# Last expert's PSUM sums moved into its first matrix, and four banks cleared earlier at the start

## The chip, the cores and the metric

One core of a Trainium2 chip runs the whole program. The metric is device time in microseconds (us) of one execution. TensorE's clock has two levels, 1.2 and 2.4 GHz; the profile gives the granted clock as a share of the upper one (0.50 or 1.00).

## The reference

One decoder layer over 256 tokens of width 1024, in float32. Two head groups share one input projection (4 heads of differential attention, 8 heads of RWKV-7 time mixing); then comes a mixture of 32 experts, 4 per token. Norms are modulated by six vectors made from a conditioning vector.

```python
mod = silu(c) @ ada_w + ada_b
sh1, sc1, gt1, sh2, sc2, gt2 = split(mod, 6)
h = rms_norm(x, pre_mix_norm) * (1 + sc1) + sh1
proj = h @ w_in
da_part, rw_part = proj[..., :DA_COLS], token_shift(proj[..., DA_COLS:], rw_mu)
lam = exp(sum(lam_q1 * lam_k1)) - exp(sum(lam_q2 * lam_k2)) + lambda_init
# attention: (softmax(q1 k1) - lam * softmax(q2 k2)) v, for each head
y = concat([diff_attention(da_part), rwkv7_time_mix(rw_part)]) @ w_out
x = x + gt1 * rms_norm(y, post_mix_norm)
h = rms_norm(x, pre_ffn_norm) * (1 + sc2) + sh2
gates = top-4 softmax of (h @ router_w + router_b)
acc = sum over e of gates[e] * (clamped_swiglu(h @ w1[e] + b1[e]) @ w2[e] + b2[e])
return x + gt2 * rms_norm(acc, post_ffn_norm)
```

## The kernel before

Weights stream from HBM through a ring of 18 slots of 1 MB in SBUF. SyncE's queue issues nearly all loads in program order; a load is issued when the slot it writes has been released by the instructions that read it. Tokens are gathered per expert into 32, 64 or 96 columns (`kind`), multiplied with the first matrix (`gemm1`, eight row blocks k of w1, which come as four loads of 2 MB, so k = 0 and 1 arrive together), put through the activation (`act_of`), transposed (`act_tr`), multiplied with the second matrix (`gemm2`, four loads of 1 MB in the order 0, 2, 1, 3), scaled by the gates into `ys`, and put back to their tokens by a matmul with `back` (`scatter`). For most experts VectorE adds the scattered rows to `acc` in SBUF. Both GEMMs take a table `between`: after row block k they call `between[k]`, which is how other work is put into TensorE's queue at a chosen place. TensorE, VectorE and ScalarE take their instructions in exactly this written order in this part of the program.

PSUM has eight banks: four named `bank`, three `bankb` and one `bankc`. For the last expert, the result is summed in PSUM: `sum_so_far(i)` (L1764) takes two banks for token tile i, and puts into each, by a matmul with the identity, what `acc` holds so far, and then by a matmul of `pgT` with `b2t` the gated biases of all second matrices. `b2t` is loaded by GpSimd (L1860) in `late_rows`, when the last expert begins. When a tile has its `ends`, `scatter` adds into these banks and VectorE has nothing to add. `last_norm` then reads them. In the kernel before, the last expert issues `warm(24)` (matmuls of ones, whose result nobody reads) behind its first matrix, and the scatter of the last expert but one and both `sum_so_far` are woven into its second matrix.

At the start, the modulation vectors are computed four times 256 columns at a time: `mod_rows` (products with `cs`, one row in each of four partition groups), `mod_copy` (VectorE copies them to SBUF), `mod_cols_first` (matmuls with `q32` that turn rows into columns, then VectorE makes scale `g1` and shift `sh1`), `mod_x` (ScalarE and VectorE apply them and split the result into a high and a low part). `col_tr(0)` transposes the small parameter vectors `prow` into columns `pc`. `split_first` splits weights in high and low parts. `proj_first` is the projection, accumulated over eight row blocks in seven banks, which are cleared beforehand by a matmul with zeros (`rwb`, L427 to L431).

Lambda of the attention is computed by five VectorE operations and an exponential on ScalarE (L729 to L736) in a part of the program that a scheduler orders; there `tc.issue_after` holds an operation back until a named one was placed.

Of the kernel before, what the change touches and what calls it, by code (L numbers as in the profile page):

```python
# [15 lines left out]
AF = mybir.ActivationFunctionType  # L16
OP = mybir.AluOpType
# [5 lines left out]
NT = 2  # L23
# [8 lines left out]
SINGLE = 4  # L32
# [14 lines left out]
MIX = "hh" "mh" "mh" "hw" + ("mm" "hm" "hw") * 2 + "mm" "mm" "hm" "mm" "hh"  # L47
MAX_OVER = 16
OVER_AT = 8
WARM = (34, 4, 0, 6, 8)  # L50
LEAD = 5
WORK = ("* * * d1 * * d2 * * * d2 * * d2 * d1 * d1 * d3 * T1 d2 T3 * T0 K0.0 d4 U0 d1 * d5 * K0.4 r0 * * T2 d2 m * * "
        "L0.0 d3 U2 K1.0 m * d4 m * q0.0 * L1.0 d4 K1.4 L0.4 d1 m m m r1 d5 d1 m q1.0 d2 q0.1 q1.1 d2 * s0.0 * "
# [22 lines left out]
def hybrid_layer_kernel(ctx, tc, x, c, positions, ada_w, ada_b, pre_mix_norm, post_mix_norm,  # L76
# [335 lines left out]
    xj = pair((1024,), (1024,))  # L412
    norm_x(xj)
    x_tr(0, xj[0])
    mod_rows(0, 0, ada)
    x_tr(1, xj[1])
    mod_rows(0, 1, ada)
    col_tr(0)
    V.tensor_scalar(pc[:, cols["sc1"][0]:cols["sc1"][0] + 8], pc[:, cols["sc1"][0]:cols["sc1"][0] + 8], 1.0, None,
                    op0=OP.add)  # L420
    mod_copy(0)
# [2 lines left out]
    for _ in range(2):  # L424
        next(sf)
    mod_cols_first(0)
    rwb = {}  # L427
    ORDER = (0, 2, 4, 6, 8, 10, 12)
    for f in ORDER:
        rwb[f] = (bankb if f in (12, 8, 10) else bank)()  # L430
        mm(rwb[f], zero, zero[:, 0:1].to_broadcast([128, 512]), True, False)  # L431
    warm(WARM[1], bankc)
    next(sf)
    mod_x(0)
    for _ in sf:
# [6 lines left out]

    mu1 = pro.tile([128, 14], F32)

    def shift(dst, p, f):
        S.activation(dst, p, AF.Copy, scale=mu1[:, f:f + 1])  # L446
        V.scalar_tensor_tensor(dst[:, 1:], p[:, 0:T - 1], col("mu", f), dst[:, 1:], op0=OP.mult, op1=OP.add)  # L447

    def proj_first(k, fs):
# [276 lines left out]
        S.activation(dst[:, :, i * 128:(i + 1) * 128], b.rearrange("p (a b) -> p a b", a=4), AF.Copy)  # L726

    lam2 = pro.tile([128, 2], F32)
    V.tensor_tensor(lamt[:, 0], lamt[:, 0], lamt[:, 1], op=OP.mult)  # L729
    V.tensor_tensor(lamt[:, 2], lamt[:, 2], lamt[:, 3], op=OP.mult)  # L730
    V.tensor_reduce(lam2, lamt[:, 0:4:2], axis=AX.X, op=OP.add)
    with tc.issue_after(first_act.ins):
        S.activation(lam2, lam2, AF.Exp)
    nlam = pro.tile([128, 1], F32)
    V.tensor_tensor(nlam, lam2[:, 1:2], lam2[:, 0:1], op=OP.subtract)
    V.tensor_scalar(nlam, nlam, LAMBDA_INIT, None, op0=OP.subtract)  # L736
    sub_c = pro.tile([128, 1], F32)
    V.tensor_scalar(sub_c, col("subln", 0), 1.0 - LAMBDA_INIT, None, op0=OP.mult)
    scs, ats = {}, {}
# [411 lines left out]
        S.activation(gT[:, f:f + 2], b.rearrange("p (a b) -> p a b", a=2), AF.Copy)  # L1151
    finish(8, 10)
    rkr, gB = rT, gT
    fill()


# [417 lines left out]
        return view(ring[n // 2][:, n % 2], shape)  # L1574


    def load_expert(e, s1_, s2_, single=False):


        w1 = moe_w1[0][e] if isinstance(e, int) else moe_w1[0][bass.ds(e, 1)].rearrange("o k n -> (o k) n")  # L1580
        w2 = moe_w2[0][e] if isinstance(e, int) else moe_w2[0][bass.ds(e, 1)].rearrange("o k n -> (o k) n")
        at = taken[0]
        taken[0] += KC + 4
        for j in range(4):

            d = ring[(at + 2 * j) % N_SLOTS // 2]
            s = w1[j * 256:(j + 1) * 256, :].rearrange("(p k) n -> p k n", k=2)
            s1_ += [d[:, 0], d[:, 1]]
            if j == 3:
                yield  # L1590
            if single:
                nc.sync.dma_start(d[:, 0], s[:, 0])
            if j == 3:
                yield
            if single:
                nc.sync.dma_start(d[:, 1], s[:, 1])
            else:
                nc.sync.dma_start(d.rearrange("p k n -> p (k n)"), s.rearrange("p k n -> p (k n)"))
        for n, k in enumerate(W2_ORDER):
            yield  # L1600
            s = s2_[k] = slot((at + KC + n) % N_SLOTS, (2, D))
            nc.sync.dma_start(s, w2[k * 256:(k + 1) * 256, :].rearrange("(p k) n -> p k n", k=2))

    def load_all(e):
        w = [], {}
# [167 lines left out]

    summed = set()

    def scatter(ys, back, which=range(NT)):
        for i in which:
            for n in range(2):
                h = slice(64 * n, 64 * n + 64)
                if i in ends:  # L1780
                    for m, (j, y) in enumerate(ys):
                        mm(ends[i][n], back[h, j, i], y[h], False, m == len(ys) - 1)
                    continue
                b = bankb()
                for m, (j, y) in enumerate(ys):
                    mm(b, back[h, j, i], y[h], m == 0, m == len(ys) - 1)
                a = acc[:, i, n * 512:(n + 1) * 512]
                if (i, n) in summed:
                    V.tensor_tensor(a, a, b, op=OP.add)  # L1789
                else:  # L1790
                    V.tensor_copy(a, b)
                    summed.add((i, n))
# [130 lines left out]
    for p in range(EXPERTS):  # L1923
        kind = kind_at(p)
        w1s, w2s = weights
        if p + 1 < EXPERTS:
            weights = [], {}
            rest_of_load = load_expert(expert_of(p + 1), *weights, p + 1 < SINGLE)
            next(rest_of_load)
        else:  # L1930
            late_rows()
        between = {}
        if p == 0:
            between = {2: order_a, 4: order_b, 5: order_c, 7: order_d}
        gemm1(bs, xs, w1s, kind, between, rest_of_load)
        act = act_of(bs, kind)
        early = p == 0 or done[2] == 96
# [28 lines left out]

            between[3], between[5] = between[5], rest_of_first
        elif not nxt:
            warm(24)
            between = {0: lambda: scatter(*done[:2], which=(0,)), 1: lambda: scatter(*done[:2], which=(1,)),  # L1970
                       5: lambda: sum_so_far(0), 3: lambda: sum_so_far(1)}
        elif not early:
            scatter(*done[:2], which=(0,))
            if p % 2:
# [10 lines left out]
            over_plan()  # L1985
        if p == OVER_AT:
            last = nc.values_load(n_ov, min_val=0, max_val=MAX_OVER)
    scatter(*done[:2])
    pe_order.close()
    last_norm(ends)  # L1990
    for i in range(NT):
# [64 lines left out]
```

## Time and profile before

| | us |
|---|---|
| median of 3 runs | 1189.94 |
| lowest and highest | 1188.75, 1190.77 |
| the profiled execution | 1190.35 |
| its span, first to last instruction | 1188.5 |
| TensorE busy in the span | 1078.3 |

An interval in the timeline is given as start and length, both in us from the span's start. Busy time of TensorE counts matmuls, also those that run at the lower clock. A time in brackets at a row's end is how long the engine was idle before it and what it waited for.

### The profile page before, as it was taken

To read this page: it belongs to the slowest core of one execution; us is meant where nothing else is said; L and a number is where in the kernel's file an instruction comes from. 1 tells how busy PE (TensorE), PEld (TensorE's weight loads), DVE (VectorE), ACT (ScalarE), POOL (GpSimd) and SP (SyncE) were. 2 spreads that over 40 slices of the span, in tenths; PEclk is the share of its full clock that TensorE was granted. 3 is DMA by queue.
4 is the path that set the end of the run, shared out by engine and by line. 5 is a ranking of instruction groups with operands and counts; after the bars stand their busy time and mean duration, and the time that the engine had idled before them with its cause. 6 is when DMAs were issued, how large, how long until landed. Compare 5 with 4: busy or idle time off the path is not lost.

```text
span 1188.5 us, 17092 instructions
## 1 busy us (share of the span) xinstructions
PE 1078.3 (91%) x6717; PEld 507.3 (43%) x6717; DVE 412.1 (35%) x1114; ACT 227.6 (19%) x529; POOL 53.7 (5%) x100
## 2 busy tenths in 40 slices
PE   8999999999997877999988999988999999798765
PEld 6976667654343232233443233433333434333211
DVE  5688469852331212122323112312212223121203
ACT  4374353312011001010111010111010101101001
POOL 1331020000000000000000000000000000000000
PEclk8999999999999988999999999999999999999978
DMA  9862778899999999999999999999999999999991
GB/s 336 317 235 71 280 270 330 326 371 383 423 424 426 426 425 426 425 426 424 425 425 426 424 426 427 422 426 426 423 426 426 425 426 425 425 426 425 423 382 48
DMA packets 60101, 453.15 MB, mean 381 GB/s; under 512 B 7850, under 2 KB 16105, under 8 KB 23154
## 3 DMA queue, kind: packets, MB, share of 16 engines
q1 hardware_dynamic: 57970, 449.88, 91.9%
q0 software_dynamic: 1856, 2.13, 0.6%
q8 instruction: 54, 0.88, 0.3%
q14 instruction: 29, 0.24, 0.1%
q10 hardware_dynamic: 192, 0.02, 0.0%
HBM read 450.94 MB, written 1.06 MB: 380 GB/s over the span
## 4 chain that ended last, share of the span: by engine, by line
DMA 45%; PE 45%; DVE 6%; ACT 2%; issue 1%; SPq 0%; DVEq 0%; ACTq 0%
DMA pair<-in_moe_w 44%; PE bank L104 32%; PE bankb L104 10%; PE bankc L104 3%; DMA pair<-in_ada_w 1%; DVE pair L316 1%; PE bank L107 1%; ACT aTt L1731 0%; PE bankb L107 0%; DVE pair L447 0%; ACT xs L1656 0%; DVE w L316 0%; DVE pair L1195 0%; ACT pair L446 0%; DVE w L766 0%
## 5 line engine op out<-in xcount | busy, mean ns | idle before, releaser
L104 PE MATMUL bank<-pair,xs 128*64 128x512 f32 (+1 forms) x2240 | 408.6, 616 | 64.2 <-DMA pair<-in_moe_w 64.1
L104 PEld LDWEIGHTS bank<-pair,xs 128*64 128x64 f32 (+1 forms) x2240 | 114.5, 127 | 346.0 <-issue 241.3
L104 PE MATMUL bank<-pair,aTt 128*64 128x512 f32 (+1 forms) x1120 | 227.9, 618 | 12.0 <-ACT aTt L1731 10.7
L1676 DVE TENSOR_SCALAR glu<-bank 128x256 f32<-128x256 f32 x55 | 23.1, 420 | 397.2 <-PE bank L104 397.1
L1679 ACT ACTIVATE act<-glu 128x256 f32<-128x256 f32 x55 | 22.9, 417 | 464.8 <-DVE glu L1676 464.8
L1789 DVE TENSOR_TENSOR acc<-acc,bankb 128x512 f32<-128x512 f32 x120 | 77.4, 681 | 94.6 <-PE bankb L104 94.6
L104 PEld LDWEIGHTS bank<-pair,aTt 128*64 128x64 f32 (+1 forms) x1120 | 53.2, 126 | 124.9 <-issue 101.2
L104 PEld LDWEIGHTS bankb<-sel,own 128*128 128x128 f32 x608 | 73.5, 198 | 14.7 <-DVE glu L1676 9.0
L104 PE MATMUL bankb<-sel,own 128*128 128x96 f32 (+3 forms) x608 | 76.4, 285 | 0.0
L1759 ACT ACTIVATE ys<-bank,gs 128x512 fp32r<-128x512 f32 x32 | 22.0, 687 | 261.2 <-PE bank L104 261.2
L1760 DVE SCALAR_TENSOR_TENSOR ys<-bank,gs,ys 128x512 fp32r<-128x512 f32 x32 | 24.0, 751 | 106.2 <-ACT ys L1759 106.2
L104 PE MATMUL bankb<-ys,back 64*128 64x512 f32 x254 | 55.8, 449 | 4.7 <-DVE acc L1789 3.5
L1656 ACT ACTIVATE xs<-bankb,s2c,g2c 128x128 f32<-128x128 f32 (+2 forms) x136 | 48.3, 436 | 42.4 <-PE bankb L104 42.4
L1651 DVE TENSOR_SCALAR back<-bankb,pcol 128x256 fp32r<-128x256 f32 x35 | 16.6, 483 | 87.6 <-PE bankb L104 87.6
L104 PEld LDWEIGHTS bankb<-ys,back 64*128 64x128 f32 x254 | 25.8, 191 | 42.3 <-issue 26.0
L104 PE MATMUL bankb<-w,w 128*128 128x512 f32 (+3 forms) x120 | 30.9, 366 | 0.0
L1731 ACT ACTIVATE aTt<-bank 128x256 f32<-128x256 f32 x55 | 19.2, 386 | 50.6 <-PE bank L107 50.4
L104 PE MATMUL bankb<-w,own 128*128 128x512 f32 x80 | 27.3, 424 | 0.0
L104 PE MATMUL bank<-own,pair 128*128 128x256 f32 x128 | 26.6, 293 | 0.0
L104 PE MATMUL bank<-pair,pair 32*32 32x32 f32 (+4 forms) x400 | 26.1, 246 | 0.1
L104 PE MATMUL bankc<-pair,cs 128*32 128x256 f32 (+1 forms) x256 | 24.6, 493 | 1.4 <-DMA pair<-in_ada_w 1.4
L107 PE MATMUL bank<-ident,act 128*128 128x128 f32 x110 | 22.4, 315 | 2.4 <-DVE act L1681 2.4
(482 smaller groups left out, 1011.0 us busy)
## 6 DMA issues: line engine op xcount, KB each, us to landing
pair<-in_moe_w SPq DMA_DIRECT2D x112, 2048.0 KB
pair<-in_moe_w SPq DMA_DIRECT2D x160, 1024.0 KB
pair<-in_ada_w SPq DMA_DIRECT2D x24, 1024.0 KB
pair<-in_w_in SPq DMA_DIRECT2D x8, 896.0 KB
pair<-in_w_in SPq DMA_DIRECT2D x6, 1024.0 KB
pair<-in_w_out SPq DMA_DIRECT2D x4, 1024.0 KB
own<-in_x SPq DMA_DIRECT2D x2, 512.0 KB
own<-in_x SPq DMA_DIRECT2D x1, 1024.0 KB
```

What stands on the lines that cost most here:

```text
L104: PE.matmul(o, l, r, start=start, stop=stop)
L107: PE.transpose(o, i, ident[0:i.shape[0], 0:i.shape[0]])
L316: last_lo = lo_eng.tensor_tensor(lo, src, hi.bitcast(F32), op=OP.subtract)
L1651: V.tensor_scalar(back[:, j], b3, pcol32[:, j:j + 1] if j or kind == 32 else pcol64, None, op0=OP.is_equal)
L1656: S.activation(xs[:, k, :cap], b, AF.Identity, scale=g2c[:, k:k + 1], bias=s2c[:, k:k + 1])
L1676: V.tensor_scalar(glu, v[:, :, 0], 7.0, None, op0=OP.min)
L1679: S.activation(dst, glu, AF.Tanh, scale=0.851)
L1731: S.activation(aTt[:, j0:j0 + 2], b[:, :256].rearrange("p (a b) -> p a b", a=2), AF.Copy)
L1759: S.activation(yh, b, AF.Copy, scale=gs[:, j:j + 1])
L1760: V.scalar_tensor_tensor(yl, b, gs[:, j:j + 1], yh.bitcast(F32), op0=OP.mult, op1=OP.subtract)
L1789: V.tensor_tensor(a, a, b, op=OP.add)
```

## The change

At the start, `col_tr(0)` goes ahead of the modulation rows, four of the seven banks are cleared ahead of the column products and three behind them, and the four warm-up matmuls behind them go. Lambda's operations move behind the last token shift. In the last expert, both `sum_so_far` and the scatter of the last expert but one are called from the first matrix (after its row blocks 1, 3 and 5), that scatter accumulates into the banks without closing the group, and `warm(24)` becomes `warm(10)`. The last slab of the last expert's second matrix is loaded in two halves (rows j = 0 and 1 of each pair, 4 KB per partition each).

```diff
-WARM = (34, 4, 0, 6, 8)
+WARM = (34, 10, 0, 6, 8)
...
     x_tr(0, xj[0])
+    col_tr(0)
     mod_rows(0, 0, ada)
     x_tr(1, xj[1])
     mod_rows(0, 1, ada)
-    col_tr(0)
+    rwb = {}
+    ORDER = (0, 2, 4, 6, 8, 10, 12)
+
+    def clear(*fs):
+        for f in fs:
+            rwb[f] = (bankb if f in (12, 8, 10) else bank)()
+            mm(rwb[f], zero, zero[:, 0:1].to_broadcast([128, 512]), True, False)
+
+    clear(*ORDER[:4])
...
     mod_cols_first(0)
-    rwb = {}
-    ORDER = (0, 2, 4, 6, 8, 10, 12)
-    for f in ORDER:
-        rwb[f] = (bankb if f in (12, 8, 10) else bank)()
-        mm(rwb[f], zero, zero[:, 0:1].to_broadcast([128, 512]), True, False)
-    warm(WARM[1], bankc)
+    clear(*ORDER[4:])
...
     def shift(dst, p, f):
-        S.activation(dst, p, AF.Copy, scale=mu1[:, f:f + 1])
+        nonlocal last_shift
+        last_shift = S.activation(dst, p, AF.Copy, scale=mu1[:, f:f + 1])
...
-    V.tensor_tensor(lamt[:, 0], lamt[:, 0], lamt[:, 1], op=OP.mult)
...
     finish(8, 10)
     rkr, gB = rT, gT
+    later = ExitStack()
+    later.enter_context(tc.issue_after(last_shift.ins))
+    V.tensor_tensor(lamt[:, 0], lamt[:, 0], lamt[:, 1], op=OP.mult)
...
+    later.close()
...
-            nc.sync.dma_start(s, w2[k * 256:(k + 1) * 256, :].rearrange("(p k) n -> p k n", k=2))
+            w = w2[k * 256:(k + 1) * 256, :].rearrange("(p k) n -> p k n", k=2)
+
+            for j in range(2) if last and n == 3 else (slice(0, 2),):
+                nc.sync.dma_start(s[:, j], w[:, j])
...
-    def scatter(ys, back, which=range(NT)):
+    def scatter(ys, back, which=range(NT), last=False):
...
-                        mm(ends[i][n], back[h, j, i], y[h], False, m == len(ys) - 1)
+                        mm(ends[i][n], back[h, j, i], y[h], False, last and m == len(ys) - 1)
...
-            rest_of_load = load_expert(expert_of(p + 1), *weights, p + 1 < SINGLE)
+            rest_of_load = load_expert(expert_of(p + 1), *weights, p + 1 < SINGLE, p + 2 == EXPERTS)
...
             between = {2: order_a, 4: order_b, 5: order_c, 7: order_d}
+        if p == EXPERTS - 1:
+            between = {1: lambda: sum_so_far(0), 3: lambda: sum_so_far(1), 5: lambda: scatter(*done[:2])}
         gemm1(bs, xs, w1s, kind, between, rest_of_load)
...
         elif not nxt:
-            warm(24)
-            between = {0: lambda: scatter(*done[:2], which=(0,)), 1: lambda: scatter(*done[:2], which=(1,)),
-                       5: lambda: sum_so_far(0), 3: lambda: sum_so_far(1)}
+            warm(WARM[1])
+            between = {}
...
-    scatter(*done[:2])
+    scatter(*done[:2], last=True)
```

TensorE's order at the start, the difference of the two kernels from the transposes of x to the column products (`prow` is the small vectors, `cs` the modulation rows' operand, `zero` a clear, `q` the column products):

```order
 L107 MATMUL bank<-ident,pair_174 128x128 x8
+L107 MATMUL bankb<-ident,prow_85 128x24
 L104 MATMUL bankc<-pair_87,cs 32x256 x8
 L107 MATMUL bank<-ident,pair_174 128x128 x8
 L104 MATMUL bankc<-pair_89,cs 32x256 x8
-L107 MATMUL bankb<-ident,prow_85 128x24
-L104 MATMUL bankc<-q_115,w_221 128x1 x4
 L104 LDWEIGHTS zero
 L104 MATMUL bank<-zero 128x512
```

The transpose of the small vectors has left the place between the modulation rows and their column products, and clears stand there now; the column products follow behind the fourth clear.

TensorE's order in the last expert's second matrix in the kernel before (`pair` with `aTt` is the second matrix, `ys` with `back` a scatter, `acc` and `pgT` a sum and its biases):

```order
L107 MATMUL bank<-ident,act 128x128 x2
L104 MATMUL bank<-pair_1159,aTt 32x512 x2
L104 MATMUL bankb<-ys,back 128x512 x4
L104 MATMUL bank<-pair_1159,aTt 32x512 x2
L104 MATMUL bankb<-ys,back 128x512 x4
L104 MATMUL bank<-pair_1159,aTt 32x512 x4
L104 MATMUL bankb<-acc,ident 128x512
L104 MATMUL bankb<-pair_776,pgT 128x512
L104 MATMUL bankb<-acc,ident 128x512
L104 MATMUL bankb<-pair_776,pgT 128x512
L104 MATMUL bank<-pair_578,aTt 32x512 x4
```

The same engine in the last expert's first matrix in the changed kernel (`pair` with `xs` is the first matrix):

```order
L104 MATMUL bank<-pair_2693,xs 32x512 x8
L104 MATMUL bankb<-acc,ident 128x512
L104 MATMUL bankb<-pair_771,pgT 128x512
L104 MATMUL bankc<-acc,ident 128x512
L104 MATMUL bankc<-pair_771,pgT 128x512
L104 MATMUL bank<-pair_2694,xs 32x512 x8
L104 MATMUL bankb<-ys,back 128x512 x6
L104 MATMUL bankc<-ys,back 128x512 x2
L104 MATMUL bank<-pair_1422,xs 32x512 x8
```

Sums, biases and scatter now stand between the pairs of the first matrix (the first sum in the same way behind the first pair), and the second matrix is eight and eight matmul rows with nothing between.

## Rows read from the trace of the kernel before

**Rows 1.** The page: GB/s in 40 slices of the span, and the chain by engine.
```profile
GB/s 336 317 235 71 280 270 330 326 371 383 423 424 426 426 425 426 425 426 424 425 425 426 424 426 427 422 426 426 423 426 426 425 426 425 425 426 425 423 382 48
...
DMA 45%; PE 45%; DVE 6%; ACT 2%; issue 1%; SPq 0%; DVEq 0%; ACTq 0%
```

**Rows 2.** The chain in order of time: start, length, what.
```profile
2.41 10.84 DMA pair<-in_ada_w
...
34.77 2.85 PE bank L104 x24
...
1120.12 31.77 DMA pair<-in_moe_w
...
1163.37 4.21 PE bankb L104 x8
```

**Rows 3.** Timeline of the last expert: start, length, engine, line, operation, idle before it.
```profile
1137.24 3.64 PE L104 MATMUL bank<-pair,xs 128*32 128x512 f32 x16 [4.28 <-DMA pair<-in_moe_w]
...
1147.04 1.92 PE L104 MATMUL bank<-pair,xs 128*32 128x512 f32 x16 [1.44 <-DMA pair<-in_moe_w]
...
1151.93 3.53 PE L104 MATMUL bank<-pair,xs 128*32 128x512 f32 x16 [2.96 <-DMA pair<-in_moe_w]
...
1155.39 2.84 PE L104 MATMUL bank<-ones 128*128 128x256 bf16 x24
...
1156.83 0.42 DVE L1681 SCALAR_TENSOR_TENSOR act<-act,lin 128x256 f32<-128x256 f32 x1
...
1159.00 1.05 PE L104 MATMUL bank<-pair,aTt 128*32 128x512 f32 x4 [0.53 <-ACT aTt L1731]
...
1159.98 0.74 PE L104 MATMUL bankb<-ys,back 64*128 64x512 f32 x4
...
1172.72 1.06 PE L104 MATMUL bank<-pair,aTt 128*32 128x512 f32 x8
```

**Rows 4.** One stretch: length, busy PE, PEld, DVE, ACT, POOL, granted clock, DMA share, GB/s.
```profile
1135.00:1140.00 5.00, 2.76 (x16) 0.60 (x16) 0.00 (x0) 0.00 (x0) 0.00 (x0) 0.50 1.00 426
```

**Rows 5.** A stretch of 1 us behind the last landing, same columns.
```profile
1161.00:1162.00 1.00, 1.00 (x8) 0.30 (x4) 1.00 (x2) 0.00 (x0) 0.00 (x0) 1.00 0.00 0
```

**Rows 6.** Timeline: load of the biases, last additions; DMA issues: time to landing.
```profile
1122.68 0.53 POOL L1860 DMA_DIRECT2D pair<-in_moe_b  x1 [0.73 <-PE bank L104]
...
1125.69 1.87 DVE L1789 TENSOR_TENSOR acc<-acc,bankb 128x512 f32<-128x512 f32 x3
...
pair<-in_moe_b POOLq DMA_DIRECT2D x1, 128.0 KB, 12.8
```

**Rows 7.** Timeline of the start.
```profile
13.29 1.07 PE L104 MATMUL bankc<-pair,cs 128*32 128x256 f32 x16 [0.78 <-DMA pair<-in_ada_w]
...
14.86 0.68 DVE L375 COPY w<-bankc 128x512 f32<-128x512 f32 x1
...
15.69 1.84 PE L104 MATMUL bankc<-q,w 128*128 128x1 f32 x8 [1.16 <-DVE w L375]
...
17.39 1.87 PE L104 MATMUL bank<-zero 128*128 128x512 bf16 x4
...
18.71 0.42 DVE L396 TENSOR_TENSOR w<-w,own 128x256 fp32r<-128x256 f32 x1 [0.21 <-ACT own L394]
...
21.04 0.56 PE L104 MATMUL bank<-own,pair 128*128 128x256 f32 x1
```

**Rows 8.** A stretch of 1 us at the start, same columns as rows 4.
```profile
22.00:23.00 1.00, 1.00 (x10) 1.00 (x9) 1.00 (x2) 0.00 (x0) 0.00 (x0) 0.85 1.11 402
```

**Rows 9.** Timeline of ScalarE and GpSimd: splits of the third w_in slab.
```profile
27.21 1.79 ACT L405 ACTIVATE pair<-pair 128x896 fp32r<-128x896 f32 x2 [5.54 <-DMA pair<-in_w_in]
...
29.08 2.10 POOL L407 TENSOR_TENSOR pair<-pair,pair 128x896 fp32r<-128x896 f32 x1 [8.22 <-ACT pair L405]
```

**Rows 10.** TensorE's longest wait from 66 to 330 us; longest of lambda's operations.
```profile
PE bank L104 <- ACT Lhl L315: 1.5, 1, 1.5
...
71.92 0.27 DVE L731 TENSOR_REDUCE lam<-lamt 128x2 f32<-128x128 f32 x1
```

## What the change will do to the time

> **What bounds the kernel now.** I read four views. The page first: over the whole span the chain that ended last is half weight transfer, half TensorE [rows 1]. Then that chain in order of time [rows 2]. The reader is to see three parts in it. In the first quarter it is TensorE, VectorE and ScalarE with one transfer, at the very start. Then it runs back and forth between TensorE and the stream of expert weights, whose last piece ends at 1151.9 us [rows 2]; the page's slices from 297 to 1129 us all move 422 to 427 GB/s [rows 1]. After 1151.9 us no weight transfer is in it: everything up to the end at 1188.5 us is compute that runs after the stream. Then the timeline of those last 50 us, and that of the first 25 us.
>
> The tail first. The last expert's four pairs of first-matrix slabs land 4.9 us apart, and a pair is 1.92 us of TensorE at 2.4 GHz, so the engine idles between them [rows 3]. The granted clock there is 0.50, the lower of its two levels, 1.2 GHz [rows 4], and a pair then takes 3.64 or 3.53 us. After the fourth pair the order on TensorE is: 24 warm-up matmuls, the transposes of the activation, then the second matrix, into which 8 scatter matmuls and 8 sum and bias matmuls are woven. The second matrix itself is four slabs of 1.05 us. The woven work is 2 x 0.74 us of scatter [rows 3] and twice 4.21 us of sums [rows 2]. The second matrix starts at 1159.00 us and ends at 1173.78 us, though the last weights are in by 1161 us: DMA moves nothing after it [rows 5]. So about 12 us between landing and end are only TensorE's queue, and the end (ys, last scatter, norm, store) follows 14.7 us later, at 1188.5 us.
>
> **The change part by part.** Sums against the profiled execution: 1190.35 us, which is its span of 1188.5 us and 1.85 us around it; the median of the runs shown is 0.41 us lower, at 1189.94 us.
>
> *Sums, biases and scatter into the first matrix.* Taken from behind the landing: 2 x 4.21 + 2 x 0.74, some 9.9 us. They are put into gaps. From 1137.24 us TensorE's list is, at the upper clock: four pairs x 1.92 = 7.7 us, sums 8.4 us, scatter 1.5 us, together 17.6 us. Without a clock loss it ends at 1154.9 us, about where the first matrix ends before (1151.93 + 3.53 = 1155.46 us), and the fourth pair, landing at 1151.93 us, is not what it waits for. But the engine comes to 1137.24 us after 4.3 us of idling, at 1.2 GHz. In the trace a busy engine got the upper level back within its next pieces: the pair at 1137.24 us ran low, the one at 1147.04 us ran high, with an idle 1.27 us between [rows 3]. Here there is no gap any more. At the start of the program it took from 15.69 us to somewhere in 22 to 23 us, 6.6 us of nearly continuous work [rows 8]. I bound the low stretch by these 6.6 us and by the 3.6 us of a first pair that runs wholly low; each microsecond of it costs half a microsecond, so 1.8 to 3.3 us, and I take 2.2 us, nearer to the pair, since it is the same place: the first matrix ends at 1157.1 us, 1.6 us later than before.
>
> The first sum needs the biases of the second matrices, loaded by GpSimd: issued at 1122.68 us and 12.8 us to landing [rows 6], so there at 1135.5 us, before the first of them is wanted (1139 us at the earliest). It also needs the accumulator, whose last additions end at 1127.6 us [rows 6]. If either were late, all four pairs behind it in TensorE's queue would wait too. Four VectorE additions go (the scatter now accumulates into PSUM); they lay beside TensorE and save nothing.
>
> *Warm-up 24 to 10.* The activation is ready at 1157.25 us [rows 3], while the 24 matmuls hold TensorE until 1158.23 us. Ten last 1.2 us and end before the activation is ready, 1.8 us after the first matrix. So from the end of the first matrix to the first product of the second it takes 1.8 + 0.5 (transposes) + 0.6 (ScalarE copy and its waits), 2.9 us, where it took 3.5 us.
>
> *The second matrix* is then 4 x 1.05 = 4.2 us: 1157.1 + 2.9 + 4.2 = 1164.2 us against 1173.78 us. **Gain at the tail 9.6 us**, 8.5 to 10.0 us by the bounds of the clock; none of what follows changes.
>
> *Last slab in two.* It matters only where TensorE waits for that slab. In the sum above TensorE reaches it at 1163.1 us, 2 us after the data's end, so I cost it at nothing. If TensorE were earlier, it lets the first half be used about 1.2 us sooner (1 MB at 425 GB/s is 2.5 us). The floor of the whole part lies there: half a slab's products behind the last landing, 1161.5 + 0.5 = 1162 us, a gain of at most 11.5 us. As a cost, the stream is made of 1024 KB and 2048 KB loads and holds its rate over both [rows 1], and no load of 512 KB is in it; queued back to back I take no loss, at most the time of half a slab, 1.2 us, which TensorE's lateness still covers. The Trainium skill (DMA: Bandwidth & Descriptors, Bandwidth) speaks against such a cut: it advises transfers of at least 1 MiB. Its fit of 2.0 us plus bytes at 436 GB/s would put two halves one behind the other about 2 us later than one slab, an estimate from that page; by it the floor would be 1164 us instead of 1162, and only the rival with the clock high at both ends would come out 2 us later.
>
> *The start: four banks cleared ahead of the columns, column transpose earlier.* Before: the modulation rows end at 13.29 + 1.07 = 14.36 us; VectorE's copy of them begins at 14.86 us, behind two small operations that waited for the column transpose; the column products start at 15.69 us, then seven clears and four warm-ups, and the projection begins at 21.04 us [rows 7], still at 1.2 GHz until 22.3 us or so [rows 8]. Its operands were ready at 19.1 us (VectorE's low part, 18.71 + 0.42). Now the copy can start at 14.45 us and end at 15.13 us. Four clears lie beside it: at the low clock 4 x 0.47 = 1.9 us, to 16.2 us, at the high one half of that, to 15.3 us. Column products 1.84 us at the low clock, to 18.05 us; from their end to the low part it is 19.13 - 17.53 = 1.6 us, with three clears (1.5 us) beside: the projection begins at 19.6 us, a gain of 1.4 us. If the clock does not fall, since the 1.16 us of idling ahead of the columns is now filled, columns end at 16.2 us, the projection begins at 17.8 us and runs high from its first product. Before, the low stretch to 22.3 us cost it 0.65 us, so this end is a gain of 3.9 us. I take the middle, **2.5 us**.
>
> Does that reach the end? From 15.69 to 67 us the chain is on TensorE alone (30 pieces, one of them in [rows 2]), so its whole list moves up. The nearest transfer: the third w_in slab is there at 27.21 us and its last split ends at 31.2 us [rows 9], and its products start at 34.77 us [rows 2], 3.6 us of room. From 66 to 330 us TensorE's waits, of which the longest in sum is 1.5 us, are all for ScalarE and VectorE, none for DMA [rows 10], and the weight loads are issued as slots come free, so the stream should start earlier by the same.
>
> *Lambda moved.* Five VectorE operations, the longest 0.27 us [rows 10], and one exponential go from about 72 us to behind the last token shift; the last two stand between mask products there. Both places are busy ones, and at most their 1 us changes place: 0.5 us either way through the order around it; I take 0.
>
> Sum: 1190.35 - 9.6 - 2.5 = 1178.25; I forecast **1178.2 us**.
>
> **The rivals.**
> *Only the tail pays.* The stream is at its full rate from 297 us, and a start earlier by 2.5 us may be lost in the scheduled middle, where small reorderings cost as much. For it: the chain runs through transfers in some 45% of the span [rows 1]. Against it: TensorE waits for none from 66 to 330 us. Then 1190.35 - 9.6 = 1180.8 us.
> *The clock helps at both ends.* It is high from the first clear and soon after 1137.24 us: 11.3 us at the tail, nearly the floor, and 3.9 us at the start: 1175.2 us. For it: there is no idling left in either place. Against it: 4.3 us of idling ahead of 1137.24 us remain.
> *The clock stays low through the last expert.* Then the 17.6 us become some 34 us, the first matrix ends at 1171.6 us, the second (8.4 us) at 1182.9 us, and the last scatter takes some 1 us more: 10 us late at the tail, and with the start's gain 1190.35 + 10 - 2.5 = 1198 us. It decides if the low level lasts over 23 us of unbroken work from 1137.24 us; before, it was over by the pair at 1147.04 us, 9.8 us later, with two idle gaps in between [rows 3]. The Trainium skill (TensorE: Matmul & The Clock Gate, Part 1) says the lower clock is the default state and activity releases it; the trace agrees in those pairs.
> *It does not do what it says*: the sums wait for a bank or the biases, and the pairs behind them pile up. The biases are there 3.5 us before they are wanted, so a delay of the whole list by 8 us would be needed for no gain: 1188 us and above.
>
> **How the numbers follow.** The forecast, both parts within their bounds: 0.61. Tail alone: 0.21. Clock at both ends: 0.12. Sums wait: 0.03, two thirds of it within 0.2% of before and one third slower. Clock low: 0.03. The range from 1174.5 to 1183.0 us reaches from just under the high-clock case to 2 us above the tail-only one. 0.2% (2.4 us) is about what a measurement of this kernel can tell from no change: faster 0.94, within it 0.02, slower 0.04.
>
> **What would show it.** Right: between the pairs of the last expert, bankb and bankc matmuls with acc and pgT where TensorE now waits for DMA; the second matrix a block of some 4.2 us with nothing between; ys on ScalarE 2.5 to 4.5 us after the last weight landed, not 12; the first projection product at 17.8 to 19.6 us, and the stream's first full slices 1.4 to 3.9 us earlier. Wrong: a granted clock of 0.50 past 1145 us, a TensorE wait in front of the first sum, or a stream that ends where it did.

## The result, and the profile after

The changed kernel takes 1176.51 us (median of 4 runs, 1174.69 to 1177.31), the kernel before 1190.24 us beside it (4 runs, 1188.75 to 1190.77): ratio 0.9885, 95% interval 0.9871 to 0.9899. The profiled execution took 1174.69 us, its span 1172.9 us. It is 15.7 us shorter than the profiled execution of before; between the two medians it is 13.7 us. The forecast was 1178.2 us. Some executions of several kernels in this document, the changed one among them, run 5 to 13 us longer than the others of the same kernel, most of them at a lower granted clock over the span, and the medians hold them all.

The page of the changed kernel, GB/s in 40 slices and the chain by engine, answers to [rows 1]:

```profile
GB/s 335 320 245 73 320 264 331 320 377 391 423 424 427 424 426 425 424 426 424 427 424 425 426 425 426 422 426 426 425 425 425 425 425 426 424 426 425 426 411 165
...
PE 46%; DMA 44%; DVE 7%; ACT 2%; issue 1%; SPq 0%; DVEq 0%; ACTq 0%
```

The last two slices show it: transfers fill 411 and 165 GB/s where they had 382 and 48, since less compute follows the stream. The chain in order of time, start and length, answers to [rows 2]:

```profile
1100.11 32.47 DMA pair<-in_moe_w
1132.62 3.64 PE bank L104 x16
1136.26 4.55 PE bankb L104 x8
...
1149.86 1.90 PE bank L104 x16
1154.62 3.69 PE bank L104 x32
```

The last transfer of the chain now ends in front of the first pair of the last expert, at 1132.6 us. Before it ended in front of the fourth, at 1151.9 us [rows 2]. From there on the chain is TensorE's own list. The timeline of the last expert (columns as in [rows 3]):

```profile
1132.62 3.64 PE L104 MATMUL bank<-pair,xs 128*32 128x512 f32 x16 [3.25 <-DMA pair<-in_moe_w]
1136.19 1.46 PE L104 MATMUL bankb<-acc,ident 128*128 128x512 f32 x2
...
1140.74 1.92 PE L104 MATMUL bank<-pair,xs 128*32 128x512 f32 x16
...
1146.81 1.92 PE L104 MATMUL bank<-pair,xs 128*32 128x512 f32 x16
...
1149.79 1.92 PE L104 MATMUL bank<-pair,xs 128*32 128x512 f32 x16
1151.64 1.26 PE L104 MATMUL bank<-ones 128*128 128x256 bf16 x10
...
1154.62 3.64 PE L104 MATMUL bank<-pair,aTt 128*32 128x512 f32 x32 [0.53 <-ACT aTt L1743]
...
1157.19 0.15 PEld L104 LDWEIGHTS bank<-pair,aTt 128*32 128x32 f32 x6 [0.29 <-DMA pair<-in_moe_w]
1158.39 0.69 ACT L1771 ACTIVATE ys<-bank,gs 128x512 fp32r<-128x512 f32 x1 [3.82 <-PE bank L104]
```

After the first pair no row of TensorE carries a wait in brackets until the warm-ups end: no sum waits for a bank or for the biases, no pair for its weights. The second matrix is one block of 32. The PEld row (PEld is TensorE loading an operand ahead of its matmuls) belongs to the products of the last half slab, and it waited 0.29 us for DMA: TensorE's queue and the stream reach their ends together. The clock, two stretches (columns as in [rows 4]):

```profile
1132.50:1136.50 4.00, 3.88 (x17) 0.91 (x18) 0.00 (x0) 0.00 (x0) 0.00 (x0) 0.50 1.02 434
...
1157.30:1158.30 1.00, 0.96 (x12) 0.05 (x6) 0.00 (x0) 0.00 (x0) 0.00 (x0) 1.00 0.00 0
```

The first pair and the beginning of the first sum ran at 1.2 GHz; the granted clock was back at 1136.9 us. From 1157.3 us on the transfers move nothing (DMA share 0.00), and the second matrix ends 1 us later; before, it ended 12 us behind the landing [rows 5]. And the start, answering to [rows 7]:

```profile
14.37 1.07 PE L104 MATMUL bankc<-pair,cs 128*32 128x256 f32 x16 [2.00 <-DMA pair<-in_ada_w]
15.37 1.04 PE L104 MATMUL bank<-zero 128*128 128x512 bf16 x4
15.51 0.69 DVE L375 COPY w<-bankc 128x512 f32<-128x512 f32 x1 [2.18 <-PE bankc L104]
16.25 1.05 PE L104 MATMUL bankc<-q,w 128*128 128x1 f32 x8
...
18.51 0.38 PE L104 MATMUL bank<-own,pair 128*128 128x256 f32 x1 [0.53 <-ACT own L394]
```

The clears lie beside VectorE's copy. The stretch from 16 to 19 us (columns as in [rows 4]):

```profile
16.00:19.00 3.00, 2.28 (x13) 1.30 (x12) 1.64 (x6) 2.29 (x5) 1.27 (x1) 1.00 1.06 361
```

The clock is at 2.4 GHz there, where before it was 0.50 from 15.5 to 22.3 us.

### The profile page after: what moved, and what is told of

It reads as the page before. It is cut to its first block, busy times and chain, and to the rows that moved or that the text cites. A ratio compares the mean times of both kernels' runs of the same rounds, so it can differ in the third digit from the quotient of the medians.

```text
span 1172.9 us, 17052 instructions
## 1 busy us (share of the span) xinstructions
PE 1069.7 (91%) x6698; PEld 502.7 (43%) x6699; DVE 409.7 (35%) x1110; ACT 227.4 (19%) x529; POOL 54.2 (5%) x100
## 3 DMA queue, kind: packets, MB, share of 16 engines
HBM read 450.94 MB, written 1.06 MB: 385 GB/s over the span
## 4 chain that ended last, share of the span: by engine, by line
PE 46%; DMA 44%; DVE 7%; ACT 2%; issue 1%; SPq 0%; DVEq 0%; ACTq 0%
DMA pair<-in_moe_w 43%; PE bank L104 32%; PE bankb L104 10%; PE bankc L104 2%; DMA pair<-in_ada_w 1%; DVE pair L316 1%; PE bank L107 1%; ACT aTt L1743 0%; ACT xs L1668 0%; PE bankb L107 0%; DVE pair L454 0%; ACT pair L1107 0%; DVE pair L1204 0%; DVE w L316 0%; DVE acc L1801 0%
## 5 line engine op out<-in xcount | busy, mean ns | idle before, releaser
L1801 DVE TENSOR_TENSOR acc<-acc,bankb 128x512 f32<-128x512 f32 x116 | 74.9, 682 | 89.5 <-PE bankb L104 89.5
L104 PE MATMUL bank<-pair,pair 32*32 32x32 f32 (+4 forms) x400 | 26.1, 246 | 0.1
```

The source lines that it names most:

```text
L104: PE.matmul(o, l, r, start=start, stop=stop)
```

## The experiments

Each was timed beside the kernel before on the same chip. The small steps are read from the profiles, since the times spread too widely for them. A code cut shows the edit against the changed kernel; "..." marks lines left out.

**Where it comes from: each part alone.** Three kernels on one chip (before: 1188.73 us). The first leaves out the start edits and lambda's, and keeps all of the last expert's:

```diff
-    col_tr(0)
     mod_rows(0, 0, ada)
...
     mod_rows(0, 1, ada)
-    clear(*ORDER[:4])
+    col_tr(0)
...
-    clear(*ORDER[4:])
+    for f in ORDER:
+        rwb[f] = (bankb if f in (12, 8, 10) else bank)()
+        mm(rwb[f], zero, zero[:, 0:1].to_broadcast([128, 512]), True, False)
+    warm(4, bankc)
```

> The kernel before with the change in the last expert alone: sums, biases and scatter called from its first matrix, 10 warm-up matmuls, last slab in two halves. Theory (the tail pays by itself what the traces show between the last landing and the end of the second matrix, 12.0 us before and 1.1 us after): 10.9 us faster than before, about 1179.3 us. Rival (part of it needs the earlier start, since the clock and the stream stand differently): 9 us or less, 1181 us or more.

Measured: 1179.67 us, ratio 0.9929 (0.9909 to 0.9949), 9.1 us below the kernel before by the medians, between the theory's 10.9 and the rival's 9. In its profile the tail is whole: the second matrix again ends about 1.1 us behind the last weights, and from the last expert's first pair to that end it takes 25.6 us, as in the changed kernel. Its start, which is the code of before:

```profile
13.73 1.07 PE L104 MATMUL bankc<-pair,cs 128*32 128x256 f32 x16 [0.81 <-DMA pair<-in_ada_w]
...
16.13 1.02 PE L104 MATMUL bankc<-q,w 128*128 128x1 f32 x8 [1.16 <-DVE w L375]
...
18.89 0.36 PE L104 MATMUL bank<-own,pair 128*128 128x256 f32 x1
```

The stretch from 16 to 19 us of the same profile:

```profile
16.00:19.00 3.00, 2.87 (x20) 2.02 (x21) 1.49 (x6) 2.33 (x5) 1.36 (x2) 1.00 1.05 358
```

Same order as [rows 7], same 1.16 us of idling ahead of the columns, and yet the clock did not fall: this stretch has 1.00, in the kernel before it has 0.50. From the second modulation rows to the projection it took 5.16 us (18.89 - 13.73) instead of 7.75. So the low stretch in the profile of before is not a property of that order; the clock falls there in some executions.

The second has the start edits alone (the piece of the change's diff from `col_tr(0)` to `clear(*ORDER[4:])`), the third the lambda edits alone (`last_shift` and the `later` block).

> The kernel before with the change at the start alone: column transpose ahead of the modulation rows, four banks cleared ahead of the columns, no four warm-ups. Theory (the start gives the 2.3 us by which the second modulation rows come earlier in the trace after, 25.96 against 28.26 us, and the other 2.3 us of the stream's 4.6 come from elsewhere): about 1187.9 us. Rival (the start gives all 4.6 us by which the last weights land earlier): about 1185.6 us.

Measured: 1188.04 us, ratio 1.0017 (0.9992 to 1.0042): no gain that can be told from none. Eight of its 12 values are 1186.0 to 1188.6 us, four 1195.6 to 1199.9.

> The kernel before with lambda's five VectorE operations and its exponential moved behind the last token shift, and nothing else. Theory (the scheduler's other order between 66 and 90 us gives 1.1 us of the stream's 4.6): about 1189.1 us. Rival (prediction: it gives nothing): 1190.2 us. Third: the order costs, 1190.7 us and above.

Measured: 1193.52 us, ratio 1.0036 (1.0012 to 1.0060), with half of the 12 values at 1186.4 to 1190.6 and half at 1196.4 to 1199.1 us. Taken for itself that makes lambda's move a loss of some 4 us, as the third expectation had it; its one profile, of an execution of 1188.64 us, doesn't show where. By their medians the three parts alone come to a gain of 5 us (9.1 + 0.7 - 4.8), far from the whole, so these medians can't be added up. The counter-test is lambda back at its old place in the changed kernel, beside the changed kernel itself, on another chip (before: 1190.0 us).

```diff
-    later.enter_context(tc.issue_after(last_shift.ins))
...
+    with tc.issue_after(first_act.ins):
+        S.activation(lam2, lam2, AF.Exp)
```

> The changed kernel with lambda's operations where they were before, so start and last expert changed alone. Theory now (moving lambda brings under 1 us; the 4.4 us by which the trace after stands ahead at 238 us are the start's own 1 us and the clock, which fell at 15, 100 and 261 us in the profiled execution of before and not in that of after): within 1 us of the changed kernel. Rival (the scheduler's new order behind the move brings 1 to 2 us): 1 to 2 us slower than the changed kernel.

> The changed kernel once more, beside the three below. Theory (the ratio 0.9885 is the change, whatever clock a single execution meets): 0.988 to 0.990 of before. Rival (the profiled execution of before was an unlucky one at the start and its luck is in the ratio): 0.992 or more.

Measured: 1177.14 us (ratio 0.9909, 0.9887 to 0.9931) with lambda back, 1178.42 us (0.9923, 0.9899 to 0.9947) for the changed kernel. In the changed kernel lambda's move is worth nothing that shows; why it measured a loss in the kernel before stays open. And the first timing's ratio of 0.9885 did not come again: 0.9923 is in the range of the rival, though its interval and the first one's (0.9871 to 0.9899) just touch. By the medians the gain is 11.6 us here, where it was 13.7 us.

**The sums.** The changed kernel, with both sums and their biases back in the second matrix; the scatter stays in the first.

```diff
-            between = {1: lambda: sum_so_far(0), 3: lambda: sum_so_far(1), 5: lambda: scatter(*done[:2])}
+            between = {5: lambda: scatter(*done[:2])}
...
-            between = {}
+            between = {5: lambda: sum_so_far(0), 3: lambda: sum_so_far(1)}
```

> The changed kernel with both sums and biases back in the last expert's second matrix; the scatter of the expert before stays in the first matrix, but goes through VectorE again. Theory (sums cost 8.4 us behind the landing, of which the 2.4 us that the first matrix then ends earlier come off): 6 us slower than the changed kernel, about 1182.5 us on the scale of the first timing. Rival (the sums were hidden anyway): no slower. Second rival (all of it shows): 8.4 us slower, 1185 us.

Measured: 1183.19 us, ratio 0.9944 (0.9929 to 0.9959), 4.8 us above the changed kernel beside it by the medians; the intervals of the two overlap, so the profile has to decide. Its last expert:

```profile
1134.19 3.64 PE L104 MATMUL bank<-pair,xs 128*32 128x512 f32 x16 [4.21 <-DMA pair<-in_moe_w]
1139.09 3.35 PE L104 MATMUL bank<-pair,xs 128*32 128x512 f32 x16 [1.26 <-DMA pair<-in_moe_w]
...
1148.93 3.55 PE L104 MATMUL bank<-pair,xs 128*32 128x512 f32 x16 [0.83 <-DMA pair<-in_moe_w]
...
1155.40 1.92 PE L104 MATMUL bank<-pair,aTt 128*32 128x512 f32 x16 [0.53 <-ACT aTt L1743]
...
1166.67 1.06 PE L104 MATMUL bank<-pair,aTt 128*32 128x512 f32 x8
```

TensorE waits between the pairs again, and the second matrix ends at 1167.7 us, 9.0 us behind the last landing (1158.71 us in its transfer records). From the first pair to that end it takes 33.5 us, 7.9 us longer than in the changed kernel, near the second rival's 8.4. So the sums in the gaps are the main part of the gain. Nearly all of their 8.4 us fits there: the second matrix starts 21.2 us after the first pair here (1155.40 - 1134.19) and 22.0 us after it in the changed kernel, so they delay it by 0.8 us. Two further pairs of this list, the second and the fourth, ran at 1.2 GHz (3.35 and 3.55 us); without gaps only the first pair did.

**The last slab.** The changed kernel with the slab in one piece.

```diff
-            for j in range(2) if last and n == 3 else (slice(0, 2),):
-                nc.sync.dma_start(s[:, j], w[:, j])
+            nc.sync.dma_start(s, w2[k * 256:(k + 1) * 256, :].rearrange("(p k) n -> p k n", k=2))
```

> The changed kernel with the last slab of the second matrix loaded in one piece. Theory (TensorE comes to this slab when all of it has landed, or within 0.2 us of that: in the trace after it starts its products at about 1157.4 us and the second half landed at 1157.2 us): no difference, 1176.5 us. Rival (the cut lets TensorE go on with half a slab): 1 us slower, 1177.5 us. Rival from the page on DMA sizes (small loads are slow): faster than the changed kernel by 1 us or more.

Measured: 1175.59 us, ratio 0.9883 (0.9865 to 0.9901), against 0.9885 in the first timing: the cut does nothing that shows. In this execution TensorE did wait for the slab:

```profile
1156.43 2.78 PE L104 MATMUL bank<-pair,aTt 128*32 128x512 f32 x24 [0.53 <-ACT aTt L1740]
1160.55 1.06 PE L104 MATMUL bank<-pair,aTt 128*32 128x512 f32 x8 [1.35 <-DMA pair<-in_moe_w]
```

The stream was late here by itself: by the transfer records the slab ahead landed 4.0 us behind the one before it (1158.06 and 1154.04 us), where 2.5 us is the rule. The whole slab's products end 1.1 us behind its landing (1160.51 us).

**Warm-ups ahead of the first matrix.** The rest of the tail that seemed open was the first pair at 1.2 GHz.

```diff
         if p == EXPERTS - 1:
+            warm(24)
             between = {1: lambda: sum_so_far(0), 3: lambda: sum_so_far(1), 5: lambda: scatter(*done[:2])}
```

> The changed kernel with 24 warm-up matmuls put ahead of the last expert's first matrix, into the 3.3 us in which TensorE waits for its first pair. Theory (the low clock at that pair costs the list some 1.8 us, but only 0.5 us of that shows, since the last weights land at 1157.2 us and the second matrix ends at 1158.3 us): the pair takes 1.9 us instead of 3.6, TensorE waits for the last slab, and the whole is 0.5 us faster, too little for the timing. Rival (the prediction's term, 2.2 us, comes back in full): 2 us faster. Second rival (the warm-ups are late themselves and push the list): 1 us slower or more.

Measured: 1175.27 us, ratio 0.9886 (0.9869 to 0.9903), 3 us below the changed kernel on the same chip. Its profile:

```profile
1129.38 2.80 PE L104 MATMUL bank<-ones 128*128 128x256 bf16 x24
1133.26 1.93 PE L104 MATMUL bank<-pair,xs 128*32 128x512 f32 x16 [1.08 <-DMA pair<-in_moe_w]
...
1153.27 1.93 PE L104 MATMUL bank<-pair,aTt 128*32 128x512 f32 x16 [0.53 <-ACT aTt L1743]
1155.37 1.06 PE L104 MATMUL bank<-pair,aTt 128*32 128x512 f32 x8 [0.18 <-DMA pair<-in_moe_w]
1156.62 1.05 PE L104 MATMUL bank<-pair,aTt 128*32 128x512 f32 x4 [0.18 <-DMA pair<-in_moe_w]
1157.86 1.05 PE L104 MATMUL bank<-pair,aTt 128*32 128x512 f32 x4 [0.19 <-DMA pair<-in_moe_w]
```

The first pair now runs high, the second matrix starts 20.0 us after it instead of 22.0, and all of that turns into waits: each of the last three pieces waits for its landing, and the end is again 1.1 us behind the last one. So this is the floor, and the changed kernel was already on it. Four matmul rows of a half slab take 1.05 us, eight of a whole one 1.06 us: in the single records the rows start four at a time, 0.45 us apart, and of a half slab only two at a time, so both take two turns. That is why the cut brings nothing even where TensorE waits for it.

Where, then, do 3 us of median come from? One explanation was that in the longer executions the low clock lasts longer in the last expert. This kernel once more, beside the changed kernel and two others, on a third chip (before: 1189.05 us):

> The changed kernel with 24 matmuls of ones ahead of the last expert's first matrix, once more, beside the changed kernel on the same chip. Theory (in a part of the executions the low clock lasts longer in the last expert and the unbroken list of the first matrix is late by it; the warm-ups end that): a median 1.5 to 3 us below the changed kernel's of this call, the first pair in 1.92 us, no upper values above 1180 us. Rival (the difference of the earlier runs was spread, the second matrix is set by the landings in both): a median within 0.7 us of the changed kernel's, with as many upper values.

> The changed kernel as it is, for comparison with the other three of this call. Both theories: a median of 1176 to 1179 us, a span of 1172 to 1175 us in the profile, 4.1 us from the second modulation rows to the first projection product, the second matrix ending about 1.1 us behind the last landing.

Measured: 1174.94 us, ratio 0.9895 (0.9865 to 0.9925), against 1178.15 us, 0.9937 (0.9906 to 0.9967). But two of its six values are above 1180 us (1181.04 and 1184.69), and the first of these is the profiled one, which shows where such an execution loses its time:

```profile
15.28 1.39 PE L104 MATMUL bankc<-pair,cs 128*32 128x256 f32 x16 [1.99 <-DMA pair<-in_ada_w]
...
18.29 1.71 PE L104 MATMUL bankc<-q,w 128*128 128x1 f32 x8
...
21.19 0.58 PE L104 MATMUL bank<-own,pair 128*128 128x256 f32 x1
...
1163.57 1.05 PE L104 MATMUL bank<-pair,aTt 128*32 128x512 f32 x4 [0.19 <-DMA pair<-in_moe_w]
```

The stretch from 16 to 19 us of this execution:

```profile
16.00:19.00 3.00, 3.00 (x16) 1.48 (x9) 0.69 (x1) 1.15 (x2) 0.86 (x1) 0.50 1.03 362
```

The end is on the same floor behind its landing. The loss is at the start: the clock fell in front of the clears and stayed at 0.50 until 26.1 us; the projection begins 3.1 us later than in the changed kernel's profile beside it (18.07 us), and the first expert's first product 4.8 us later (242.90 against 238.09 us). So the theory of a longer low stretch in the last expert falls for this execution. That its medians were 3 us lower on these two chips (9 of the 12 values are below 1175.8 us, of the changed kernel's 17 only 3) is measured, but nothing ties it to the warm-ups: on the third chip the two kernels described next have no warm-ups there and measured 1175.45 and 1176.16 us, also under the changed kernel's 1178.15 us, the first of them with a longer tail. No profile shows the cause, and it stays open.

**Warm-ups behind the first matrix.** 24 instead of 10, on the third chip.

```diff
-            warm(WARM[1])
+            warm(24)
```

> The changed kernel, with 24 matmuls of ones behind the last expert's first matrix instead of 10. Theory (TensorE's queue sets the time from the first matrix to the second): the second matrix starts 3.5 to 3.6 us behind the first instead of 2.98 us, and the time is 0.6 us longer. Rival (the transfers set the end of the second matrix, the warm-ups lie beside them): the second matrix ends as far behind the last landing as without them, 1.1 us, and the time is the same. Second rival (the warm-ups keep the clock up in the second matrix): its products drop below 3.64 us and the time falls.

Measured: 1175.45 us, ratio 0.9883 (0.9865 to 0.9901). The times do not resolve 0.6 us; the profile does:

```profile
1152.66 2.79 PE L104 MATMUL bank<-ones 128*128 128x256 bf16 x24
...
1156.22 3.64 PE L104 MATMUL bank<-pair,aTt 128*32 128x512 f32 x32 [0.53 <-ACT aTt L1743]
```

3.56 us between them, against 2.98 (1154.62 - 1151.64), and the second matrix ends 1.8 us behind the last landing (1158.09 us). It takes 3.64 us in both. The first theory holds in the profile: these 14 matmuls cost 0.6 us, and buy no clock.

**Clears back behind the columns,** with the early column transpose kept and no warm-ups, on the same chip.

```diff
-    clear(*ORDER[:4])
...
-    clear(*ORDER[4:])
+    for f in ORDER:
+        rwb[f] = (bankb if f in (12, 8, 10) else bank)()
+        mm(rwb[f], zero, zero[:, 0:1].to_broadcast([128, 512]), True, False)
```

> The changed kernel, with all seven clears behind the column products as before, and without the four warm-up matmuls; the column transpose stays early. Theory (the clears ahead of the columns fill TensorE's idle time): from the second modulation rows to the first projection product 5.0 to 5.2 us with the clock high and about 7.4 us with it low, instead of 4.1 us, so 1.0 to 3.4 us longer in time. Rival (the early column transpose alone brings it, since it lets VectorE's copy start earlier): 4.1 to 4.4 us, and a time within 0.4 us of the changed kernel's.

Measured: 1176.16 us, ratio 0.9889 (0.9871 to 0.9908): by its time nothing is lost, against the theory's 1.0 to 3.4 us. Its start:

```profile
13.14 1.07 PE L104 MATMUL bankc<-pair,cs 128*32 128x256 f32 x16 [0.74 <-DMA pair<-in_ada_w]
15.02 1.15 PE L104 MATMUL bankc<-q,w 128*128 128x1 f32 x8 [0.82 <-DVE w L375]
16.04 1.87 PE L104 MATMUL bank<-zero 128*128 128x512 bf16 x4
...
18.62 0.77 PE L104 MATMUL bank<-own,pair 128*128 128x256 f32 x1
```

The stretch from 16 to 19 us of this execution:

```profile
16.00:19.00 3.00, 2.78 (x8) 1.26 (x10) 2.57 (x6) 2.87 (x7) 2.34 (x2) 0.50 1.07 351
```

5.48 us from the modulation rows to the projection, with a low stretch of 3.4 us in it, against 4.13 us beside it; its first expert's first product is 0.6 us later (238.67 against 238.09 us). The early transpose let the copy start 0.1 us after the rows' end and cut the idling ahead of the columns from 1.16 to 0.82 us. Most of the 1.35 us is clock: the clears ran at 1.2 GHz, four of them in 1.87 us. At 2.4 GHz the seven took 1.5 us (17.01 to 18.53 us in the profile of the last expert's change alone), and with that, an estimate, the projection would begin 4.4 us after the rows. That is the upper end of the rival's 4.1 to 4.4 us, so the rival is not ruled out. By this estimate the place of the clears is worth some 0.3 us at the high clock, and the early transpose and the missing warm-ups the rest of the 1.0 us between the old and the new start.

## Why the prediction came out right, and where it was off

The spans of the two profiles differ by 15.6 us (1188.5 - 1172.9): 10.9 us at the tail, counted from the first pair of the last expert to the end of its second matrix (25.6 us instead of 36.5 us), and 4.6 us by which that pair starts earlier (1132.62 against 1137.24 us). The tail's part comes again: 36.5 to 36.6 us in the profiles of the start alone and lambda alone, 25.6 to 25.7 us in the two further ones of the changed kernel. The 4.6 us depend on the execution: with the old start, in the profile of the last expert's change alone, that pair started at 1134.66 us, 2.6 us earlier than in the profile of before.

*Sums and scatter into the first matrix.* Right, and shown for the sums by taking them back out; the scatter's 1.5 us were not tested apart. The list from the first pair to the warm-ups took 19.0 us (1151.64 - 1132.62); forecast were 17.6 + 2.2 = 19.8. The clock's loss was bounded rightly: the low level was over 4.3 us after the first pair began, and cost about 2 us (estimated 2.2): the first pair took 3.57 us up to the next piece where the second took 1.85, the first sum 4.55 us where the second took 4.22. For the clock's return the forecast had read two pairs of before; the one between them ran low as well:

```profile
1142.15 3.45 PE L104 MATMUL bank<-pair,xs 128*32 128x512 f32 x16 [1.27 <-DMA pair<-in_moe_w]
```

There the clock came back only 8.0 us after the first pair began, with gaps between the pairs. So filling the gaps also brought the clock back sooner; the last section has the other profiles.

*Warm-up 24 to 10.* 2.98 us from matrix to matrix, forecast 2.9; the experiment gives the 0.6 us for itself.

*The second matrix is then 4 x 1.05.* Here the term was mis-sized: 3.64 us. The 1.05 us of a slab by itself hold the end of its last matmul, which a block pays once, not four times: in the single records of the block the rows start four at a time, 0.43 us apart, and the last four end 0.59 us after their start. The 0.8 us by which the list was shorter is of the same kind (pairs 1.85 us apart where 1.92 was counted, the scatter 1.1 us instead of 1.5). Together that makes the tail 10.9 instead of 9.6 us.

*Last slab in two: nothing.* Right in time, wrong in the floor. I put it half a microsecond behind the last landing; it is 1.1 us, with or without the cut, since a half slab takes as many turns on TensorE as a whole one. The gain at the tail was thus at its floor already, where the forecast left 2 us of room. The Trainium skill (DMA: Bandwidth & Descriptors, Bandwidth) advises transfers of at least 1 MiB, and by that page's fit the cut would cost about 2 us, an estimate. That is not borne out in this place, where SyncE's loads are queued back to back: the two halves land at 1155.91 and 1157.15 us, the first 1.24 us behind the slab of 1154.67 us and the second 1.24 us behind the first, together as much as one slab.

*The start, 2.5 us.* The projection began 2.5 us earlier (18.51 against 21.04 us) and the stream followed, by 4.4 us at the first expert. But that this is the forecast's number is luck: the term was the wrong kind of number. With the clock high in both orders the new one is worth 1.0 us (4.14 against 5.16 us from the modulation rows to the projection); with it low in both, 1.4 to 2.1 us (5.65 and 5.91 against 7.34 and 7.75 us in two profiles each, with low stretches of unlike length). All else in the 3.6 us between the profiles of before and after is that the clock fell in the one execution and not in the other. I had read the low stretch in [rows 8] as a consequence of the idling in front of the columns, which the change fills; the kernel with the old start ran through the same idling at 2.4 GHz. Nor does the new order keep it up for sure: of ten profiles with the clears ahead, one had it low under the modulation rows, two between these and the projection, and three more at the projection's beginning. By time, the start alone could not be told from nothing.

*Lambda: nothing.* Right in the changed kernel, as far as the times tell; in the kernel before its move alone measured a loss that nothing here explains.

*The sum.* The tail was forecast 1.3 us too small (9.6 for 10.9) and the start 1.5 us too large (2.5 for the 1.0 us that the order gives at the high clock). The two errors cancel, so part of the closeness of 1178.2 to 1176.5 us is luck. The repeats of the changed kernel gave 1178.42 and 1178.15 us, 11.6 and 10.9 us below the kernel before, about the tail alone.

*The signs.* The sums stood between the pairs, no sum waited, and the projection began at 18.51 us, all as set down. ScalarE's `ys` came 1.2 us behind the last landing, sooner than the 2.5 to 4.5 us, and the stream 4.4 us earlier instead of 1.4 to 3.9.

*The rivals.* That only the tail pays was the nearest to the truth in kind: its kernel measured 9.1 us below the one before, for a forecast 9.6. High clock at both ends is near what the profile of after shows, 1174.69 us for 1175.2, with the first pair low after all; the median lies between the two rivals, as the forecast did. The sums waited for nothing, and the clock came back in 4.3 us.

Left open: what the start is worth over many executions (between nothing and 3 us), what decides whether the clock falls there, why lambda's move alone measured a loss, and why the changed kernel's medians on the second and third chip lie 1 to 3 us above those of most of its variants.

## What to carry to other kernels

Work that doesn't need the last weights belongs in the gaps between the transfers ahead of them; look for it in what TensorE does after the last landing, and stop when the end is the products of one slab (1.1 us here) behind the stream, since from then on a faster TensorE only waits. A low clock in one profile is one execution's: before it goes into a sum as a gain, see whether the same code shows it in a second one. Split an operation's duration into what each further one adds and what is paid once, before multiplying it.

## What the runs showed of the hardware

- 32 matmul rows of 32 columns took 3.64 us in one block, 8 took 1.06 us and 4 took 1.05 us behind a wait.
- Two loads of 512 KB at the end of the stream landed 1.24 us apart, one of 1 MB 2.45 us behind the one before it.
- The same first 240 us of code, from the first instruction to the first expert, took 237.3 to 242.9 us in eight profiles (the changed kernel three times, and five of its variants that differ only in the last expert); the longest had the clock at 0.50 from 15.9 to 26.1 us, three of 238.2 to 239.2 us for 3.4 us between 15.6 and 22.5 us, the four others, 237.3 to 238.1 us, not in that stretch.
- In the last expert the granted clock was back at 1.00 within 3.9 to 5.1 us of the first pair's beginning in the eight profiles with the sums between the pairs and no warm-ups ahead, and within 7.8 to 8.8 us in the four with gaps of 1.25 to 1.55 us between the first three pairs.
